# Two, four and three more places between reading an inverse back and transposing it, in a hybrid decoder step

## The chip, the cores and the metric

The kernel runs on one core of a Trainium2 chip. The metric is the device time in microseconds of one execution; a median over a few runs is compared. The profile is of one further execution.

## The reference

One layer of a decoder for 256 prompt tokens and 8 single new tokens: half-step SwiGLU, then two head groups side by side (sliding-window attention with sinks, and RWKV-7 time mixing), an output projection, a second half-step SwiGLU and a norm. All in float32.

```python
x = x + 0.5 * swiglu(rmsnorm(x, n1), f1g, f1u, f1d)
proj = rmsnorm(x, nm) @ w_in
o_att = attend(q, k, v, sinks)                    # window 128, 16 heads, 4 kv heads
for t in range(T):                                # RWKV-7, 16 heads of 64
    sa = S @ (-kk[t])
    S = S * exp(logw[t]) + outer(sa, kk[t] * a[t]) + outer(v[t], k[t])
    y[t] = S @ r[t]
x = x + concat(o_att, groupnorm_gate(y)) @ w_out
x = x + 0.5 * swiglu(rmsnorm(x, n2), f2g, f2u, f2d)
```

The kernel doesn't run the recurrence token by token for the prompt. It cuts 256 tokens into four pieces of 64. In a piece, the effect of the tokens on each other is a lower triangular system, so each head and piece needs the inverse of a unit triangular 64 x 64 matrix; its two 32 x 32 diagonal blocks are inverted by elimination, the block off the diagonal by two products.

## The kernel before, in words

**The stream of weight chunks.** All big products (gu and dn of both SwiGLUs, win, wout) go through `gemm`: 1304 chunks of 128 x 512 weights (some narrower). For each, the queue of SyncE (SP) loads `raw` (six buffers), ScalarE (ACT) rounds it to `hi`, VectorE (DVE) subtracts to get `lo` (four buffers of each; from the query tiles on, and for wout, every second `lo` is GpSimd's, POOL), and TensorE (PE) does twelve products of 128 x 264, three for each of four 128-column slices, into a bank `acc`. Buffers of `raw` come free with `lo`, those of `hi` and `lo` with the chunk's products.

**The mixing stage** (768 to 1180 us of the span) does win (38 tiles of four chunks) and wout. Everything else of the stage is written as generators, `tick`ed once after every chunk; a `yield` is one place in the program, and `pause(n)` is n places. They are:

- `prep`, for each pair of heads: decays, keys and the Gram products (`gm` is their masked copy, TensorE's products are called `kr,bk`), which SP writes to DRAM (`sa`). After that come transposes of `kr` and `bk` (L515, L522) and a product `uv,gm`.
- `chain`, for each of four batches of two pairs. It waits for its `prep`s; it reads the matrices back from `sa` into `X` with one matrix row group to a partition, and POOL copies to `Xt`; it pauses DWAIT = 8 places; 30 steps of elimination follow, two a place, each a product `st` and an addition to `Xt` on VectorE. The inverse is written to DRAM (`sb`, four writes, L580), and after one place read back into `TT` in the layout for products (four reads, L585; the first and third hold what is transposed). After DWAIT - 2 = 6 places VectorE transposes the two halves, `TN` from `TT` (L591). Then TensorE multiplies `TN,gm`, and `TT,zs`, ScalarE copies the results, TensorE multiplies `kr,TT`, then with `W` (L639) come products `BT,W`, `gm,W`, `uv,BT` and `gm,uv`; VectorE scales `N`; three steps of state (`Z`, `S`) follow, and a group norm into `y`.
- attention, softmax and the decode tokens' part, in the last third of the stage.

`mp()` gives the small products one of five PSUM banks (NM = 5), `acc()` one of three.

**What sets the order.** Each engine and each queue works in order. The program order is not the final order: a scheduler puts each instruction on its engine's queue by its own estimates, and moves instructions at high priority (the chunk preparation) ahead. `tc.issue_after(cuts[0])` keeps a step of elimination and each transpose behind the newest `lo` of VectorE. So a place more in one generator moves other generators' instructions too.

Of the kernel before, what the change touches and what calls it, by code (L numbers as in the profile page):

```python
# [30 lines left out]
NWARM = 10  # L31
NGM, NKR, NUV, NTT, NBT = 10, 5, 3, 2, 5
NSTEP = 2
DWAIT = (8, 8, 8, 8)
PW = (2, 1, 3, 2, 2)
ALPHA = math.exp(-0.5)
LKV = 26
# [10 lines left out]
def body(tc, I, O):  # L48
# [42 lines left out]
    def pause(n):  # L91
        for _ in range(n):
            yield

    with ExitStack() as ctx:
# [264 lines left out]
        def mixing_body(mx, n2, n3, XD):  # L360
# [3 lines left out]
            def ring(shape, tag, bufs):  # L364
                return mx.tile(list(shape), F32, tag=tag, bufs=bufs, name=uid(tag))
# [172 lines left out]
            def newbatch(i):  # L538
                bt = Batch()
                n = BATCH[i]  # L540
                bt.i, bt.n, bt.left, bt.p0 = i, n, n, sum(BATCH[:i])
                bt.KR, bt.bv = [None] * n, [None] * n
                bt.Gm = [[None, None] for _ in range(n)]
                bt.BT = [None] * n
                bt.UV = ring((P, 4, n, P), "uv", NUV)
                return bt

            def chain(bt):
# [15 lines left out]
                for h in range(2):  # L564
                    G.memset(TT[h * 64 + 32:h * 64 + 64, :, 0:32], 0.0)
                yield from pause(DWAIT[bt.i])
                for s in range(1, 31):
# [14 lines left out]
                for h in range(2):  # L582
                    for blk in range(2):
                        x = h * 64 + blk * 32
                        SP.dma_start(TT[x:x + 32, :, blk * 32:blk * 32 + 32],  # L585
                                     scr2[bt.i].rearrange("(h b m) (s t) -> h b s m t", h=2, b=2, s=32)[h, blk])
                yield from pause(DWAIT[bt.i] - 2)
                TN = ring((P, n * 4, 32), "TN", 1)
                for h in range(2):
                    with tc.issue_after(cuts[0]):  # L590
# [286 lines left out]
            for kind, i in SEQ:  # L877
                if kind == "b":
                    bt = newbatch(i)
                    for k in range(BATCH[i]):  # L880
                        p = bt.p0 + k
                        x = [shifted(2 + 3 * p + j, tmp()) for j in range(3)]
                        spawn(prep(p, bt, k, *x))
                    bat.append(spawn(chain(bt)))
                    bts.append(bt)
                    if len(bat) == len(BATCH):
# [206 lines left out]
```

## Time and profile before

| what | value |
|---|---|
| median of 3 runs | 2002.0 us (2001.74 to 2003.65) |
| the profiled execution, whole | 1999.97 us |
| its span | 1997.9 us |
| TensorE busy | 1967.1 us, 98% |
| VectorE, ScalarE, GpSimd busy | 65%, 53%, 17% |
| DMA | 358.24 MB, mean 179 GB/s |

In the rows, `acc<-s,hi` names the result and the operands of an instruction, buffer numbers left out. The time in brackets is how long the engine stood idle before a row, and who ended it. SPq is SyncE's queue, whose rows are DMA issues and not transfers. PEclk is the granted TensorE clock, 1.00 for full.

### The profile page before, as it was taken

What the parts mean: (1) busy time and instruction counts of PE and PEld (TensorE: products, weight loads), DVE (VectorE), ACT (ScalarE), POOL (GpSimd) and SP (SyncE); (2) the same over time, 40 slices, a digit from 0 to 9 for tenths busy, and PEclk for the clock granted to TensorE, in tenths of its full rate; (3) what the DMA queues carried; (4) which work ended last, traced back from release to release, by engine and by line L of the source; (5) the groups of instructions that cost most, each with busy time, mean ns of one, the idle gap of its engine ahead of it and who ended that gap; (6) DMA issues with size and microseconds to landing.
All of it is one profiled execution on the core that took longest, in us unless ns stands there. A gap on an engine that the chain in (4) does not pass through costs nothing.

```text
span 1997.9 us, 45891 instructions
## 1 busy us (share of the span) xinstructions
PE 1967.1 (98%) x17212; PEld 1937.1 (97%) x17212; DVE 1305.4 (65%) x2542; ACT 1067.7 (53%) x2127; POOL 344.9 (17%) x453
## 2 busy tenths in 40 slices
PE   9999999999999999999899999999999999999997
PEld 9999999999999999999788899999999999999997
DVE  5865555655556567789677676766666666666655
ACT  5644444444444456776556765654444444444445
POOL 0401001010010122221134553220101001010012
PEclk9999999999999999999899999999999999999999
DMA  7666666655556567554455546565666666666654
GB/s 231 178 192 193 183 193 191 182 184 177 187 177 184 182 196 222 164 158 124 132 156 144 162 143 196 174 182 175 193 186 191 182 191 192 183 191 181 197 177 144
DMA packets 224880, 358.24 MB, mean 179 GB/s; under 512 B 38264, under 2 KB 79888, under 8 KB 224656
## 3 DMA queue, kind: packets, MB, share of 16 engines
q1 hardware_dynamic: 218768, 349.20, 58.4%
q10 hardware_dynamic: 5888, 6.11, 1.0%
q8 instruction: 135, 2.21, 0.5%
q14 instruction: 89, 0.73, 0.1%
HBM read 347.06 MB, written 10.22 MB: 179 GB/s over the span
## 4 chain that ended last, share of the span: by engine, by line
PE 94%; DVE 2%; DMA 2%; ACT 1%; SPq 1%; issue 0%; POOL 0%; DVEq 0%; ACTq 0%; POOLq 0%
PE acc L74 86%; PE m L74 7%; DMA TT<-sb 1%; DVE Xt L58 1%; DVE lo L58 0%; DMA raw<-in_gu 0%; DMA sb<-Xt 0%; DVE st L58 0%; DMA raw<-in_win 0%; ACT t L68 0%; DVE y L58 0%; DMA s<-xsp 0%; ACT hi L127 0%; DVE gm L58 0%; PE m L522 0%
## 5 line engine op out<-in xcount | busy, mean ns | idle before, releaser
L127 ACT CAST hi<-raw 128x512 fp32r<-128x512 f32 (+2 forms) x1304 | 779.0, 601 | 813.3 <-PE acc L74 721.4
L58 DVE TENSOR_TENSOR lo<-raw,hi 128x512 fp32r<-128x512 f32 (+1 forms) x1248 | 857.2, 691 | 540.6 <-ACT hi L127 511.7
L74 PE MATMUL acc<-s,hi 128*128 128x264 f32 x5940 | 1112.5, 287 | 3.0 <-ACT s L917 2.4
L74 PEld LDWEIGHTS acc<-s,hi 128*128 128x128 f32 x5940 | 926.5, 189 | 9.7 <-ACT s L917 2.6
L74 PE MATMUL acc<-s,lo 128*128 128x264 f32 x2970 | 849.4, 287 | 0.0
L74 PEld LDWEIGHTS acc<-s,lo 128*128 128x128 f32 x2970 | 560.6, 189 | 3.0 <-issue 0.7
L74 PE MATMUL acc<-t,hi 128*128 128x264 f32 x2752 | 502.8, 284 | 0.0
L74 PEld LDWEIGHTS acc<-t,hi 128*128 128x128 f32 x2752 | 425.9, 188 | 0.0
L74 PE MATMUL acc<-t,lo 128*128 128x264 f32 x1376 | 388.6, 284 | 0.0
L58 POOL TENSOR_TENSOR t<-t,t 128x264 f32<-128x264 f32 (+1 forms) x148 | 151.1, 1021 | 1149.6 <-ACT hi L127 817.6
L74 PEld LDWEIGHTS acc<-t,lo 128*128 128x128 f32 x1376 | 258.1, 188 | 0.1
L74 PE MATMUL acc<-y,hi 128*128 128x264 f32 x648 | 124.1, 285 | 0.0
L74 PEld LDWEIGHTS acc<-y,hi 128*128 128x128 f32 x648 | 101.0, 188 | 0.2
L74 PE MATMUL acc<-y,lo 128*128 128x264 f32 x324 | 92.0, 284 | 0.0
L58 DVE TENSOR_TENSOR t<-acc,t 128x264 f32<-128x264 f32 x156 | 67.4, 432 | 36.8 <-PE acc L74 36.6
L58 POOL TENSOR_TENSOR lo<-raw,hi 128x512 fp32r<-128x512 f32 x56 | 73.8, 1319 | 65.9 <-ACT hi L127 38.5
L58 POOL TENSOR_TENSOR o<-o,o 128x264 f32<-128x264 f32 x43 | 36.4, 847 | 186.2 <-ACT o L68 182.2
L74 PE MATMUL acc<-o,hi 128*128 128x264 f32 x324 | 63.2, 285 | 0.0
L74 PEld LDWEIGHTS acc<-y,lo 128*128 128x128 f32 x324 | 60.9, 188 | 0.0
L61 DVE SCALAR_TENSOR_TENSOR s<-acc,s 128x264 f32<-128x264 f32 x96 | 40.6, 427 | 16.0 <-PE acc L74 15.5
L74 PEld LDWEIGHTS acc<-o,hi 128*128 128x128 f32 x324 | 50.2, 188 | 0.0
L74 PE MATMUL m<-s,hi 128*128 128x264 f32 x260 | 48.3, 285 | 0.0
(251 smaller groups left out, 1337.8 us busy)
## 6 DMA issues: line engine op xcount, KB each, us to landing
raw<-in_gu SPq DMA_DIRECT2D x688, 256.0 KB, 3.4
raw<-in_dn SPq DMA_DIRECT2D x224, 256.0 KB, 2.9
raw<-in_win SPq DMA_DIRECT2D x152, 256.0 KB, 3.5
raw<-in_dn SPq DMA_DIRECT2D x160, 192.0 KB, 2.7
raw<-in_wout SPq DMA_DIRECT2D x48, 256.0 KB, 3.5
raw<-in_wout SPq DMA_DIRECT2D x32, 128.0 KB, 3.3
s<-xsp SPq DMA_DIRECT2D x16, 132.0 KB, 3.9
ld<-in_sT SPq DMA_DIRECT2D x16, 128.0 KB, 3.5
```

What stands on the lines that cost most here:

```text
L58: return e.tensor_tensor(out=out, in0=a, in1=b, op=op)
L61: return V.scalar_tensor_tensor(out=out, in0=a, scalar=s, in1=b, op0=op0, op1=op1)
L74: TE.matmul(out, lhsT, rhs, start=start, stop=stop, **k)
L127: A.copy(hi[:, :w], raw[:, :w])
```

## The change

The pause between the four reads and the transposes has a table of its own, RWAIT, with 8, 10, 9 and 6 places in place of 6 in each batch.

```diff
-DWAIT = (8, 8, 8, 8)
+DWAIT, RWAIT = (8, 8, 8, 8), (8, 10, 9, 6)
...
-                yield from pause(DWAIT[bt.i] - 2)
+                yield from pause(RWAIT[bt.i])
                 TN = ring((P, n * 4, 32), "TN", 1)
                 for h in range(2):
                     with tc.issue_after(cuts[0]):
                         V.transpose(TN[h * 64:h * 64 + 32], TT[h * 64:h * 64 + 32, :, 0:32])
```

The scheduler makes more of it than a shift. The first place is batch 1 on VectorE, from the last step of the elimination (`Xt_12573`) to the transposes. Before:

```order
L58 TENSOR_TENSOR Xt_12573<-Xt_12573,st_13573 128x8
L58 TENSOR_TENSOR pj_10572<-acc_13673,rs 128x264
L58 TENSOR_TENSOR lo_13893<-raw_13891,hi_13892 128x512
L58 TENSOR_TENSOR lo_13972<-raw_13970,hi_13971 128x512
L591 STREAM_TRANSPOSE TN_13848<-TT_12582 32x256 x2
L58 TENSOR_TENSOR lo_14048<-raw_14046,hi_14047 128x512
```

After, the rows from that step on, and those up to the transposes:

```order
L58 TENSOR_TENSOR Xt_12573<-Xt_12573,st_13573 128x8
L58 TENSOR_TENSOR pj_10570<-acc_13341,rs 128x264
L58 TENSOR_TENSOR lo_13634<-raw_13632,hi_13633 128x512
...
L58 TENSOR_TENSOR lo_13850<-raw_13848,hi_13849 128x512
...
L58 TENSOR_TENSOR lo_13868<-raw_13866,hi_13867 128x512
L58 TENSOR_TENSOR XD<-t_13329 128x8
L58 TENSOR_TENSOR gm_13576<-m_13539,C 128x512
L58 TENSOR_TENSOR lo_13926<-raw_13924,hi_13925 128x512
L58 TENSOR_TENSOR lo_13964<-raw_13962,hi_13963 128x512
L591 STREAM_TRANSPOSE TN_13980<-TT_12582 32x256 x2
```

Between the two stood three rows, two of them `lo`; now there stand 36, with eleven `lo` and two reciprocals. The elimination ends at an earlier chunk (eight chunks), the transposes come one chunk later.

The second place is the same batch on SP's queue, the writes `sb` and the reads `TT`. Before:

```order
L509 DMA sa_10583<-gm_13576 32x4x32 x2
L580 DMA sb_10586<-Xt_12573 256x1x32 x4
L126 DMA raw_14305<-in_win 128x512
L561 DMA X_13654<-sa_10583 32x1024
L585 DMA TT_12582<-sb_10586 32x8x32 x2
L126 DMA raw_14349<-in_win 128x512
L585 DMA TT_12582<-sb_10586 32x8x32 x2
```

After:

```order
L580 DMA sb_10586<-Xt_12573 256x1x32 x2
L126 DMA raw_13830<-in_win 128x512
L580 DMA sb_10586<-Xt_12573 256x1x32 x2
L126 DMA raw_13848<-in_win 128x512
L585 DMA TT_12582<-sb_10586 32x8x32 x4
```

The reads stood behind the fifth and the sixth raw after that of the `lo` ahead of the transposes (`raw_13970`); now they stand behind `raw_13848`, three raws ahead of it. In batch 2 the queue has four writes, the load of the cached keys (`uv<-in_kc`, L815), one raw and then the four reads, five raws earlier than before, and both transposes follow the same chunk's `lo` as the first did; from the elimination's end to them VectorE has 27 rows, five of them `lo`, one a reciprocal, twelve of `Z` and `S`.

The third place is TensorE in batch 1, where `N` is read, with the last of the products `gm,uv` ahead. Before:

```order
L74 MATMUL m_14095<-gm_12494,uv_11359 64x64
L74 MATMUL acc_14249<-s_10205,hi_14306 128x264
L74 MATMUL acc_14249<-s_10206,hi_14306 128x264
L74 MATMUL m_14157<-N_13992,PT_13991 64x64 x2
L74 MATMUL m_14095<-kr_12303,N_13992 64x64 x2
```

After:

```order
L74 MATMUL m_14244<-gm_12494,uv_11359 64x64
L74 MATMUL acc_14583<-s_10120,hi_14632 128x264
...
L74 MATMUL acc_14583<-s_10291,hi_14664 128x264
L74 MATMUL m_14302<-N_14139,PT_14138 64x64 x2
L74 MATMUL m_14244<-kr_12303,N_14139 64x64 x2
```

Two chunk products stood between, now twelve. The batch's `TN,gm` products stand in one group with the next pair's `XD,ld`, `kr,bk`, `C,kr` and `C,bk`; `TT,zs`, `kr,TT`, `BT,W` and `N` follow two, four, five and six chunks behind them. In batch 0 the `TN,gm` products likewise stand in the group of the next pair's `XD,ld` and `kr,bk`, four chunks later than before; in batch 2 they come three chunks later, five chunks behind the `lo` that the transposes follow; in batch 3 eleven behind it. Batch 3's elimination starts two chunks later, and its reads stand one to two raws later. The instructions are the same ones, but for two of ScalarE's table loads fewer (31 for 33).

## The prediction

> **What bounds the kernel now.** I read the page first, then busy time and granted clock by stretch, then TensorE's idle rows in order of time, and last VectorE's and the DMA queue's rows around the transposition.
>
> ```profile
> span 1997.9 us, 45891 instructions
> PE 1967.1 (98%) x17212; PEld 1937.1 (97%) x17212; DVE 1305.4 (65%) x2542; ACT 1067.7 (53%) x2127; POOL 344.9 (17%) x453
> PEclk9999999999999999999899999999999999999999
> ```
>
> TensorE bounds the kernel. It is idle for 30.8 us of the span, so a change of order can win only a part of that, and the time that matrix products lose when the granted clock drops. The clock row has its one dip in the slice from 949 us on, which is in the mixing stage. By stretch (TensorE busy is the first number after the length, PEclk the granted clock):
>
> ```profile
> core 0: us, PE busy (x) PEld busy (x) DVE busy (x) ACT busy (x) POOL busy (x), PEclk, DMA share, GB/s
> 895.00:920.00 25.00, 23.85 (x429) 21.25 (x427) 22.71 (x71) 15.25 (x44) 5.12 (x15) 0.93 0.50 139
> 920.00:945.00 25.00, 25.00 (x204) 24.25 (x204) 21.94 (x57) 19.92 (x45) 3.81 (x11) 1.00 0.42 119
> 945.00:965.00 20.00, 16.89 (x204) 15.68 (x203) 11.70 (x33) 13.66 (x34) 2.77 (x12) 1.00 0.67 169
> 965.00:990.00 25.00, 20.57 (x356) 18.61 (x356) 22.51 (x76) 12.36 (x34) 5.02 (x13) 0.85 0.44 126
> 990.00:1015.00 25.00, 25.00 (x212) 23.65 (x209) 18.95 (x49) 18.29 (x41) 1.84 (x10) 0.94 0.38 109
> 1015.00:1040.00 25.00, 21.34 (x232) 19.94 (x231) 12.74 (x24) 10.01 (x27) 8.57 (x13) 0.93 0.65 175
> 1040.00:1070.00 30.00, 27.00 (x387) 24.62 (x387) 27.08 (x98) 16.95 (x42) 13.27 (x19) 0.89 0.42 125
> ```
>
> Two losses are to be seen. TensorE is idle for 1.15, 3.11, 4.43, 3.66 and 3.00 us in five of these stretches, and every such stretch, or the one behind it, runs below the full clock: length times (1 - clock) is 1.75, 3.75, 1.5, 1.75 and 3.3 us. These are the idle rows (in brackets the idle time ahead, and who ended it):
>
> ```profile
> 904.75 0.71 PE L74 MATMUL m<-t,C 128*128 128x280 f32 x2 [0.47 <-POOL shc L407]
> 906.38 0.60 PE L74 MATMUL m<-kr,TT 64*64 64x64 f32 x4 [0.35 <-ACT TT L621]
> 907.21 1.48 PE L74 MATMUL m<-kr,TT 64*64 64x64 f32 x52 [0.23 <-ACT TT L621]
> 962.45 0.22 PE L74 MATMUL m<-TN,gm 32*32 32x32 f32 x2 [1.72 <-DVE TN L591]
> 964.06 0.45 PE L74 MATMUL m<-TN,gm 32*32 32x32 f32 x30 [1.39 <-DVE TN L591]
> 982.03 1.15 PE L74 MATMUL m<-gm,uv 128*64 128x64 f32 x32 [0.84 <-DVE gm L58]
> 987.21 0.37 PE L74 MATMUL m<-N,PT 64*64 64x64 f32 x2 [3.59 <-DVE N L58]
> 1027.26 1.11 PE L522 MATMUL m<-C,bk 128*128 128x128 f32 x4 [3.66 <-DVE t L58]
> 1055.66 1.62 PE L74 MATMUL m<-s,o 64*128 64x256 f32 x6 [3.00 <-DVE st L58]
> ```
>
> That a lower clock is lost time is shown by the chain of work: a run of chunk products takes 0.122 us each before the first batch's stall (7.68 / 63) and 0.187 right behind the second's (4.87 / 26):
>
> ```profile
> 801.51 7.68 PE acc L74 x63
> 964.50 4.87 PE acc L74 x26
> ```
>
> So a stall in this stage costs its length and some 1.7 us behind it (3.4 us at half clock; 1.75 in two of the stretches above), or twice that.
>
> **The wait that the change is about.** VectorE's and the queue's rows, batch 0 (895), batch 1 (953 to 964) and batch 2 (1014 to 1027):
>
> ```profile
> 895.39 0.43 DVE L591 STREAM_TRANSPOSE TN<-TT 32x256 f32<-32x256 f32 x1 [2.35 <-DMA TT<-sb]
> 953.10 0.17 DVE L58 TENSOR_TENSOR Xt<-Xt,st 128x8 f32<-128x8 f32 x1
> 954.03 2.53 SPq L580 DMA_DIRECT2D sb<-Xt  x4
> 957.97 0.80 SPq L585 DMA_DIRECT2D TT<-sb  x2
> 959.31 0.92 SPq L585 DMA_DIRECT2D TT<-sb  x2
> 961.87 0.43 DVE L591 STREAM_TRANSPOSE TN<-TT 32x256 f32<-32x256 f32 x1 [6.37 <-DMA TT<-sb]
> 963.57 0.44 DVE L591 STREAM_TRANSPOSE TN<-TT 32x256 f32<-32x256 f32 x1 [1.27 <-DMA TT<-sb]
> 1014.55 0.17 DVE L58 TENSOR_TENSOR Xt<-Xt,st 128x8 f32<-128x8 f32 x1
> 1026.71 0.43 DVE L591 STREAM_TRANSPOSE TN<-TT 32x256 f32<-32x256 f32 x1 [3.75 <-DMA TT<-sb]
> ```
>
> From the last step of the elimination to the transpose that waits, the way through DRAM takes 961.87 - 953.27 = 8.6 us for the first half and 10.3 for the second in batch 1, and 12.0 in batch 2, where weight loads stand between the writes. VectorE stands still for 7.6 and 3.75 us of it, in order, with everything behind the transpose held: the next lo, the t, gm and N that TensorE asks for.
>
> **The change part by part.** A pause issues nothing, and no DMA or product is added or taken away, so nearly all of it is order. ScalarE loads its tables 31 times for 33, 1.28 us each, of time in which it is idle nearly half (53% busy): 0 on the end.
>
> ```profile
> 888.21 1.28 ACT L68 ACT_TABLE_LOAD   x1
> ```
>
> Batch 1 (+4). The orders above show the elimination's last step eleven lo ahead of the transposes, two before, and the four reads on the queue behind the raw of the lo that is four ahead of the transpose, where two of them were behind a raw whose buffer (one of six) the lo right ahead of the transpose sets free. Between the last step and the transpose VectorE now has eleven lo, two reciprocals and 23 smaller steps. By these rows (a lo lasts 0.68 us, the next starts 0.60 after it):
>
> ```profile
> 965.46 1.79 DVE L441 RECIPROCAL t<-m 128x264 f32<-128x264 f32 x1
> 968.66 0.68 DVE L58 TENSOR_TENSOR lo<-raw,hi 128x512 fp32r<-128x512 f32 x1
> 969.26 0.42 DVE L58 TENSOR_TENSOR t<-t,t 128x264 f32<-128x264 f32 x1
> 987.95 0.47 DVE L61 SCALAR_TENSOR_TENSOR S<-m,wc,Z 128x64 f32<-128x64 f32 x2 [0.36 <-PE m L74]
> ```
>
> 11 x 0.60 + 2 x 1.75 + 23 x 0.35 = 18 us, more than the way's 10.3. The wait goes: TensorE's 1.72 + 1.39 and the 1.7 of clock behind it, **-4.8**.
>
> The backlog of batch 1. In 965 to 990 VectorE is busy for 22.51 of 25 us, and TensorE waits 0.84 for gm and 3.59 for N, with only two chunk products between the products that feed N and those that read it. In the new order twelve chunk products stand there (12 x 0.122 = 1.5 us), TN, TT, W and N are spread over chunks, and the held-up 7.6 us are gone. I take both waits and the clock lost around them (3.75 + 1.5 less the 1.7 just counted, 3.5) as won: **-7.9**. The ends are 0, if the elimination of batch 2 alone makes N late, and 7.9; I take the upper, since the missing 7.6 us of VectorE exceed the 4.4 of waiting.
>
> Batch 2 (+3). Both transposes stand together after the lo they had before; the four writes and then the reads go out five raws earlier. VectorE has five lo, a reciprocal, twelve steps of Z and S and nine others from the last step on: 3.0 + 1.75 + 12 x 0.24 + 9 x 0.4 = 11.2 us, against 8.6 and 10.3. This is close, and the load of cached keys (L815) now stands between writes and reads, so up to some 3 us of VectorE's wait may stay; TensorE's products of TN come five chunks later, 5 x 12 x 0.122 = 7.3 us, which hides that. What TensorE waited for was t behind the transpose: 3.66 + 1.7, **-5.4**.
>
> The 3.00 us at 1055.66 and 3.3 of clock: VectorE is full there (27.08 of 30) with batch 3's elimination, N of batch 2 and q. The new order starts that elimination later and spreads it over more lo. Ends 0 and -6.4; nothing in the trace says which, so half, **-3.2**.
>
> Batch 0 (+2): its first transpose goes one lo and some 3.6 us of work later. VectorE's 2.35 us go, but no TensorE row waits for it, so 0; the second transpose may wait up to 1.7 us for its read (issued at 895.20, 3.94 to landing in the chain), with the chunks that are prepared ahead (four hi and lo buffers) as cover. Batch 3 (+0): its reads go out one to two raws later with its transpose in place; bounded by 0 and batch 2's 3.75 of VectorE, hidden, since TensorE's TN products stand eleven chunks behind it.
>
> What comes back: wherever products of a batch stand close together, short waits remain, as in batch 0, which never waited for TN: 0.47 + 0.35 + 0.23 and 1.75 of clock, 2.8 us. Batch 1 and 2 will each have one such: **+5.5**; ends 0 and twice that.
>
> Sum: -4.8 - 7.9 - 5.4 - 3.2 + 5.5 = -15.8. The profiled execution took 1999.97 us round its span of 1997.9, so 1984.2 there; it lies 2.0 below the median of the runs, 2002.0, from which I take the same: **1986.2 us**.
>
> The Trainium skill, TensorE: Matmul & The Clock Gate, "Why this matters for your kernels", has the clock fall for idle gaps of more than about 3 us between bursts of products. The trace agrees for the gaps of 3.00, 3.59 and 3.66 us, and not for batch 0, where 1.05 us in three pieces stand beside a clock of 0.93. By that rule batch 1's TN waits (1.72 and 1.39) would be worth 3.1 and what comes back 2.1, and the sum would be -17.5, that is 1984.5.
>
> **The rivals.**
>
> A, only the direct waits go. The backlogs before N and q are VectorE's load, not its delay, and stay. For it: 22.51 of 25 and 27.08 of 30. Against: the standing still ahead of the first. -4.8 - 5.4 + 5.5 = -4.7: 1997.3.
>
> B, nothing: the reads are moved along by the queue and land as late against the transpose as before. For it: batch 2's 11.2 against 10.3. Against: batch 1's 18. The waits of 3.1 and 3.7 stay: 2002.
>
> C, all goes, with nothing back: -4.8 - 7.9 - 5.4 - 6.4 = -24.5: 1977.5. For it: the stretch 920 to 945 is full at a clock of 1.00 while batch 0's recurrence runs.
>
> D, slower: the five banks that the small products share. In the new order batch 0's and batch 1's TN products stand in the same group as the next pair's kr,bk, and each takes a bank that the transposes of bk wait for; that is the wait of 1027.26. At both places 5.4, and N late behind each as in batch 1 before, 7.9: +26.6 against gross gains of 21.3, 2007.3. It decides from 21.3 us of new waits. Against it: in the stretches up to 895 such groups ran without idle time.
>
> **How the numbers follow.** About 0.2% (4 us) is what a measurement of this kernel can tell from no change. Forecast 0.48, A 0.22, B 0.10, C 0.13, D 0.07. Faster: 0.48, 0.13, two thirds of A (its 4.7 is near the bound) and 0.02 of B, 0.78; slower 0.06 of D and 0.02 of B, 0.08; the rest, 0.14, the same. Range: down to C's 1977.5, up to 1999 between A and B; outside lie most of B, D and a little of C.
>
> **What would show it.** Right: no idle time before TN for a DMA in batch 1 on VectorE, under 3 us in batch 2; no TensorE wait for TN; none over 1 us for N and for bk's transposes; a granted clock of at least 0.95 in the stretch of batch 1. Wrong: TensorE waits of over 3 us at new places in the mixing stage, for gm, t or N, with the dips of the clock behind them, or a load queue that waits for TensorE at L815 while chunks run out.

## The result and the profile after

The changed kernel takes 1983.66 us (median of 5 runs, 1982.53 to 1985.16) against 2001.74 for the kernel before (5 runs in turn, 1997.97 to 2003.65): ratio 0.9911, 95% interval 0.9899 to 0.9922, 18.1 us less. The forecast was 1986.2. The profiled execution took 1982.98 us around a span of 1981.2.

The page's first lines and its clock row, after:

```profile
span 1981.2 us, 45886 instructions
PE 1960.8 (99%) x17212; PEld 1931.5 (97%) x17212; DVE 1302.9 (66%) x2542; ACT 1064.1 (54%) x2125; POOL 347.8 (18%) x453
PEclk9999999999999999999999999999999999999998
```

The dip of the slice from 949 us on is gone. The same stretches as before, after the change:

```profile
895.00:920.00 25.00, 24.95 (x427) 23.35 (x427) 22.32 (x71) 16.88 (x48) 8.90 (x17) 1.00 0.62 173
920.00:945.00 25.00, 23.97 (x225) 22.56 (x222) 22.43 (x63) 18.44 (x42) 3.70 (x13) 1.00 0.41 103
945.00:965.00 20.00, 20.00 (x189) 18.81 (x188) 14.29 (x34) 11.89 (x26) 4.79 (x11) 1.00 0.69 193
965.00:990.00 25.00, 25.00 (x404) 23.59 (x404) 23.24 (x78) 19.34 (x52) 4.48 (x10) 1.00 0.58 154
990.00:1015.00 25.00, 23.78 (x277) 22.15 (x272) 20.63 (x48) 16.36 (x39) 7.47 (x15) 1.00 0.51 144
1015.00:1040.00 25.00, 25.00 (x317) 23.32 (x316) 16.89 (x53) 17.57 (x48) 11.69 (x18) 1.00 0.59 161
1040.00:1070.00 30.00, 26.40 (x312) 23.37 (x311) 23.24 (x89) 14.51 (x42) 8.82 (x12) 0.94 0.54 146
```

The clock is full in six of the seven, and TensorE is busy throughout where batch 1 had cost most (945 to 990). TensorE's idle rows of over 0.3 us between 768 and 1180 are four, where there were ten:

```profile
922.89 0.27 PE L74 MATMUL m<-N,PT 64*64 64x64 f32 x2 [1.03 <-DVE Xt L58]
994.36 0.27 PE L74 MATMUL m<-N,PT 64*64 64x64 f32 x2 [1.22 <-DVE Xt L58]
1048.64 0.27 PE L74 MATMUL m<-N,PT 64*64 64x64 f32 x2 [3.60 <-DVE st L58]
1091.50 0.39 PE L74 MATMUL acc<-s,hi 128*128 128x264 f32 x1 [0.83 <-POOL s L58]
```

All that are over 1 us are now waits for `N`, in each of batches 0 to 2. VectorE's transposes, batch by batch:

```profile
897.39 0.42 DVE L591 STREAM_TRANSPOSE TN<-TT 32x256 f32<-32x256 f32 x1
899.86 0.43 DVE L591 STREAM_TRANSPOSE TN<-TT 32x256 f32<-32x256 f32 x1 [1.71 <-DMA TT<-sb]
957.84 0.89 DVE L591 STREAM_TRANSPOSE TN<-TT 32x256 f32<-32x256 f32 x2
1008.73 0.89 DVE L591 STREAM_TRANSPOSE TN<-TT 32x256 f32<-32x256 f32 x2
1065.61 0.95 DVE L591 STREAM_TRANSPOSE TN<-TT 32x256 f32<-32x256 f32 x2 [0.37 <-DMA TT<-sb]
```

VectorE stands still 2.1 us behind the reads in all, 13.7 before. Where the time came from: the first product of the second SwiGLU, just behind the mixing stage, before and then after:

```profile
1227.16 0.41 PE L74 MATMUL acc<-y,hi 128*128 128x264 f32 x2
```

```profile
1211.51 0.41 PE L74 MATMUL acc<-y,hi 128*128 128x264 f32 x2
```

The stage had started 0.55 us later than before (long run of chunk products from 68.49, before from 67.94), so it is 16.2 us shorter, nearly all of the span's 16.7. TensorE's busy time in 768 to 1180, before and then after, shows how much of that is idle time:

```profile
768.00:1180.00 412.00, 393.61 (x4322) 366.41 (x4321) 313.57 (x855) 280.34 (x698) 125.52 (x225) 0.97 0.53 151
```

```profile
768.00:1180.00 412.00, 405.08 (x4455) 378.59 (x4454) 323.31 (x871) 285.93 (x718) 140.49 (x238) 1.00 0.56 158
```

405.08 - 393.61 = 11.5 us of idle time, which leaves about 4.7 of the 16.2 for everything else, the clock among it, if idle time counts in full. Length times (1 - clock) over the seven stretches falls from 12.0 to 1.8, by 10.2. Both can't count in full, and the runs don't settle how the 16.2 us divide: a slow period can hold idle time too, which is then counted twice.

### The profile page after: what moved, and what is told of

It is laid out like the page before. It is cut to its first block, busy times and chain, and to the rows that moved or that the text cites. A ratio compares the mean times of both kernels' runs of the same rounds, so it can differ in the third digit from the quotient of the medians.

```text
span 1981.2 us, 45886 instructions
## 1 busy us (share of the span) xinstructions
PE 1960.8 (99%) x17212; PEld 1931.5 (97%) x17212; DVE 1302.9 (66%) x2542; ACT 1064.1 (54%) x2125; POOL 347.8 (18%) x453
## 4 chain that ended last, share of the span: by engine, by line
PE 96%; DVE 1%; DMA 1%; ACT 1%; issue 0%; SPq 0%; POOL 0%; DVEq 0%; ACTq 0%; POOLq 0%
PE acc L74 88%; PE m L74 7%; DMA raw<-in_gu 1%; DVE lo L58 0%; DVE Xt L58 0%; DVE st L58 0%; DMA TT<-sb 0%; DVE y L58 0%; DMA raw<-in_wout 0%; DMA raw<-in_win 0%; ACT t L68 0%; PE m L786 0%; PE m L522 0%; ACT L68 0%; ACT hi L127 0%
```

## The experiments

Each kernel was timed in turn with the kernel before (medians of 4 to 11 runs; ratios with 95% intervals). The theory of the prediction is called **own place**: a batch's wait goes with more places of its own behind its reads, and what TensorE lost behind it was VectorE's standing still. Against it stood **order**: places of one batch move the next batch's elimination, and what counts is where the reads go out. Chunks are counted below by the `raw` loads from the program's start, from 0.

**One batch at a time.** `RWAIT` alone is changed, in this order: (8, 6, 6, 6), (6, 10, 6, 6), (6, 6, 9, 6) and (6, 10, 9, 6).

```diff
-DWAIT, RWAIT = (8, 8, 8, 8), (8, 10, 9, 6)
+DWAIT, RWAIT = (8, 8, 8, 8), (8, 6, 6, 6)
```

> Places 8, 6, 6, 6: only batch 0's two more. Theory 'own place' (a batch's wait goes because its own transposes come later): batch 0 never held up TensorE, so nothing: -2 to +2 us against before, and VectorE still waits some 7.6 us before batch 1's transposes. Theory 'order' (what counts is how many lo stand between the elimination's last step and the transposes, and batch 0's places move batch 1's elimination ahead: here it ends seven lo ahead of batch 1's transposes, where it was two): batch 1's VectorE wait falls below 2 us, no TensorE wait for TN, -12 to -18 us.

> Places 6, 10, 6, 6: only batch 1's four more. Own place: batch 1's waits go, -4.8 directly and -7.9 with the backlog. Order: batch 1's elimination still ends at the same chunk as before, three lo ahead of the transposes, and its reads stand where they stood, so VectorE still waits 5 to 7 us there; but TensorE's TN products come six chunks behind the transposes, where they stood one ahead of them, so TensorE itself doesn't wait: -5 to -12 us, and a VectorE wait that costs nothing.

> Places 6, 6, 9, 6: only batch 2's three more. Own place: batch 2's 3.7 us wait and the clock behind it go, -5.4. Order: nothing of batch 1 changes, and batch 2's elimination, reads and transposes stand at the same chunks as before, so -2 to +2 us with VectorE's waits of 7.6 and 3.7 us as they were.

> Places 6, 10, 9, 6: the change without batch 0's two. Own place: as the change, -16 to -19. Order: batch 1's reads stand as before (VectorE still waits 5 to 7 us there), so as with batch 1's four alone, -5 to -12 us: what batch 0's two add to the whole is the rest, 6 to 13.

Measured: 0.9935 (0.9922 to 0.9947) for batch 0 alone, 0.9966 (0.9954 to 0.9978) for batch 1 alone, 1.0006 (0.9997 to 1.0015) for batch 2 alone, 0.9916 (0.9903 to 0.9930) without batch 0: 13 us and 7 us faster, nothing, 17 us faster.

Own place falls. The batch for which it expected nothing gives the most, and batch 2's places alone give nothing. With batch 0's two places alone, batch 1's transposes stand at 947.78 and don't wait, and with batch 1's four alone they still do. VectorE, in the first and then in the second kernel:

```profile
947.78 0.89 DVE L591 STREAM_TRANSPOSE TN<-TT 32x256 f32<-32x256 f32 x2
```

```profile
962.74 0.43 DVE L591 STREAM_TRANSPOSE TN<-TT 32x256 f32<-32x256 f32 x1 [3.35 <-DMA TT<-sb]
963.80 0.44 DVE L591 STREAM_TRANSPOSE TN<-TT 32x256 f32<-32x256 f32 x1 [0.63 <-DMA TT<-sb]
...
1066.95 0.43 DVE L591 STREAM_TRANSPOSE TN<-TT 32x256 f32<-32x256 f32 x1 [3.03 <-DMA TT<-sb]
1070.66 0.43 DVE L591 STREAM_TRANSPOSE TN<-TT 32x256 f32<-32x256 f32 x1 [2.42 <-DMA TT<-sb]
```

In the orders, two places more in batch 0 end batch 1's elimination at lo 626 for 634, and its reads go out behind raw 634 for 641. Four places more in batch 1 leave that as it was; they move TensorE's `TN` products from chunk 635 to 643, so that TensorE no longer waits for `TN` though VectorE does. So either edit alone takes TensorE's wait for `TN` away. They also put batch 3's reads behind raw 685 to 687 with its transposes at lo 681: the wait moves there. Batch 2's three places mend that (reads behind 685, 17 us instead of 7). So the places of one batch are worth what they do to the next, and they don't add up: 13 + 7 + 0 against 18 for all. Order was right on this, but too low for the fourth kernel. That one leaves VectorE standing for 3.7 us in batch 1 and is as fast as the whole change within the intervals. So standing still can't be all.

**Standing still, by itself.** Before's numbers, without the reads: the inverse is missing from this kernel's result, and all else runs.

```diff
-for h in range(2):
-    G.memset(TT[h * 64 + 32:h * 64 + 64, :, 0:32], 0.0)
+G.memset(TT, 0.0)
...
-SP.dma_start(TT[x:x + 32, :, blk * 32:blk * 32 + 32], scr2[bt.i]...)     # four in a batch
```

> Before's numbers; the four reads of the returned inverse per batch are left out (its tile is set to zero instead), so the transposition waits for no DMA; the inverse in the result is missing. Standing still (what TensorE lost for gm, N and t around batches 1 and 2 comes from VectorE standing in order behind the reads): all of those waits go, 14 to 22 us faster. Own load (N and t are late because the elimination and the prep fill VectorE there, reads or not): only the direct TN waits and their clock go, 3 to 6 us faster, with waits of 3 us for N and t still there.

Measured: 1991.47, ratio 0.9948 (0.9934 to 0.9961), 10 us faster, between the two. No transpose waits, and yet TensorE waits longer for `N` of batch 1 than before (3.59):

```profile
977.03 1.15 PE L74 MATMUL m<-gm,uv 128*64 128x64 f32 x32 [1.60 <-DVE gm L58]
983.88 0.37 PE L74 MATMUL m<-N,PT 64*64 64x64 f32 x2 [5.26 <-DVE N L58]
```

So the wait for `N` doesn't need VectorE's standing still. (Leaving out the reads moves the order a little too: the largest piece in the table below has 18 steps for 16.)

**The same places for batch 1, reached another way.** Batch 0's elimination starts two places later, all numbers behind the reads stay 6.

```diff
-DWAIT, RWAIT = (8, 8, 8, 8), (8, 10, 9, 6)
+DWAIT, RWAIT = (10, 8, 8, 8), (6, 6, 6, 6)
```

> All four numbers behind the reads are 6 as before; instead batch 0's elimination starts two places later (10 for 8 ahead of it). Batch 1's elimination then ends at lo 625 for 634 and its reads go out behind raw 633 with the transposition at lo 633 (before: raw 641 and 642, lo 635 and 636). Order (what counts is how many raw loads lie between the reads and the lo that the transposition stands behind; up to 3 ahead cost nothing, 5 or 6 cost 4 to 8 us of VectorE): no wait in any batch, 11 to 17 us faster. Own place (a batch's wait goes only with more places of its own behind the reads): no change, within 3 us of before.

Measured: 1996.71, ratio 0.9975 (0.9965 to 0.9984), 5 us faster, between the two ranges. Batches 1 to 3 have no wait behind the reads, as order said (batch 0's has, 3.73 us), but there is the other wait again:

```profile
991.25 0.37 PE L74 MATMUL m<-N,PT 64*64 64x64 f32 x2 [5.17 <-DVE N L58]
```

This kernel and the one with batch 0's places alone have the same order around batch 1 (elimination to lo 625 or 626, reads behind raw 633 or 634, transposes at lo 633, `N` at lo 646). They differ in batch 2's elimination: behind one `lo` stand up to 19 of its 30 steps here, up to 9 there, and TensorE waits 5.17 and 1.33 us for `N` of batch 1. That is the third theory, **burst**: `N` is late by the steps that stand in one piece ahead of it. (TensorE's rows differ too, which is taken up below the table.) In the kernel before, the largest piece is 16 steps; VectorE has no `lo` between these rows, and `N` stands at the end of the steps:

```profile
975.52 0.68 DVE L58 TENSOR_TENSOR lo<-raw,hi 128x512 fp32r<-128x512 f32 x1
...
976.87 0.20 DVE L58 TENSOR_TENSOR st<-X,Xt 128x52 f32<-128x52 f32 x1
...
985.72 0.21 DVE L58 TENSOR_TENSOR Xt<-Xt,st 128x55 f32<-128x55 f32 x1
985.86 0.61 DVE L58 TENSOR_TENSOR kr<-m,kr 128x192 f32<-128x192 f32 x2
986.39 0.68 DVE L58 TENSOR_TENSOR N<-m,wc 128x512 f32<-128x512 f32 x1
```

A step is two instructions and some 0.5 us. In the changed kernel at most eight stand behind one `lo`.

**The change without batch 1's places**: `RWAIT` (8, 6, 9, 6).

> The change without batch 1's four places (8, 6, 9, 6). Raw of the reads less lo of the transposition: 0 in batch 1, -1 in batch 2, 2 to 3 in batch 3. Order: no DMA wait of VectorE above 0.5 us in any batch, 13 to 18 us faster than before, as the whole change. Own place: batch 1's 12.7 us (direct waits and backlog) stay, 3 to 6 us faster.

Measured: 1986.04, ratio 0.9925 (0.9912 to 0.9937), 15 us faster, with no wait behind the reads in batches 1 to 3, and 1.33 us for `N` of batch 1. Most of what the prediction gave to batch 1's four places comes without them.

**Batch 2's elimination four places earlier**, most of it in one piece: before's numbers, `DWAIT` (8, 8, 4, 8).

> Before's numbers behind the reads (6, 6, 6, 6); batch 2's elimination starts four places earlier (4 for 8). Batch 1 stands as before (reads behind raw 641, transposition at lo 635 and 636); batch 2's reads go out behind raw 651, its transposition stands at lo 653, so it does not wait, but 24 of its 30 steps now stand on VectorE behind one lo (16 before, 8 in the change), ahead of N of batch 1. Burst (N of a batch is late by the steps of the next batch's elimination that stand in one piece ahead of it: 8 or 9 steps 0.9 to 1.3 us, 16 steps 3.6, 18 or 19 steps 5.2): TensorE waits 6 us or more for N of batch 1, which eats what batch 2's reads give: between 3 us faster and 5 us slower. Reads alone (only VectorE's standing behind the reads counts): batch 2's 3.66 us and their clock go, 4 to 7 us faster.

Measured: 1994.61, ratio 0.9967 (0.9954 to 0.9979), 6.6 us faster. The wait for `N` grew, to a little less than expected, but the time came out as reads alone had it:

```profile
990.21 0.37 PE L74 MATMUL m<-N,PT 64*64 64x64 f32 x2 [5.56 <-DVE Xt L58]
...
1050.32 0.37 PE L74 MATMUL m<-N,PT 64*64 64x64 f32 x2 [4.25 <-DVE st L58]
```

The 3.66 us at batch 2's `C,bk` are gone. TensorE's busy time in 768 to 1180 rises by only 1.3 us (394.91 for 393.61). The profiled span is 5.8 us shorter (1992.1 for 1997.9), but 2.2 of that lie behind the mixing stage: the first product of the second SwiGLU comes only 3.6 us earlier (1223.60 for 1227.16). From there to the end the traces of all these kernels take between 768.5 and 772.0 us. Where the other two in the stage come from isn't settled. So the wait for `N` and what the reads cost are two things.

**Ten places in all batches**: `RWAIT` (10, 10, 10, 10).

> Ten places in all four batches. Raw of the reads less lo of the transposition: 0 or 1, -2, 0 or 1 in batches 1 to 3; most steps of the next batch's elimination behind one lo: 8, 7, 13. Reads and burst: no DMA wait of VectorE in batches 1 to 3 and N of batch 1 within 1.3 us, so as the change or up to 4 us more for batch 3's 13 steps: 1982 to 1988. Set of numbers (the gain hangs on two, four and three just so): 1990 or more.

Measured: 1983.23, ratio 0.9911 (0.9897 to 0.9924): as the change. No transpose waits anywhere; `N` of batch 1 waits 1.41 us, a little over what was expected. The gain doesn't hang on two, four and three. Nor is it measured by idle time alone: in 768 to 1180 TensorE is busy for 400.40 us here and 405.08 in the changed kernel, so it idles 4.7 us more, at the same time for the whole.

All kernels, by the size of batch 2's largest piece (counted in the orders), the waits of VectorE behind the reads in batches 1, 2 and 3, and TensorE's waits in us:

| kernel | steps | reads, batch 1 / 2 / 3 | `N` of batch 1 | at 1044 to 1060 | ratio |
|---|---|---|---|---|---|
| all ten | 7 | 0 / 0 / 0 | 1.41 | 3.30 | 0.9911 |
| the change | 8 | 0 / 0 / 0.4 | 1.22 | 3.60 | 0.9911 |
| without batch 0 | 8 | 3.7 / 0 / 0.9 | 0.87 | 3.20 | 0.9916 |
| batch 1 alone | 8 | 4.0 / 0 / 5.5 | 0.87 | 2.65 | 0.9966 |
| without batch 1 | 9 | 0 / 0 / 0 | 1.33 | 3.29 | 0.9925 |
| batch 0 alone | 9 | 0 / 0 / 0 | 1.33 | 3.37 | 0.9935 |
| before | 16 | 7.6 / 3.8 / 0 | 3.59 | 3.00 | 1 |
| batch 2 alone | 16 | 7.7 / 3.1 / 0 | 3.60 | 5.12 | 1.0006 |
| no reads | 18 | none | 5.26 | 2.98 | 0.9948 |
| elimination 0 later | 19 | 0 / 0 / 0 | 5.17 | 3.66 | 0.9975 |
| elimination 2 early | 24 | 7.4 / 0 / 0 | 5.56 | 4.25 | 0.9967 |

The wait for `N` of batch 1 goes with the piece and not with the reads: 0.9 to 1.4 us for 7 to 9 steps, 3.6 for 16, 5.2 to 5.6 for 18 and more. But the piece isn't all that differs between the two groups. Between the last `gm,uv` and `N` the traces of the first six kernels show eleven or twelve chunk products on TensorE, those of the last five two or three. And of the steps only those count that VectorE does behind this `gm,uv`, whose result `N` scales: three or four in the first six, five and a half in before and batch 2 alone, nine in no reads and elimination 0 later, ten of the 24 in elimination 2 early. The rows in the changed kernel, TensorE's and then VectorE's:

```profile
990.38 1.10 PE L74 MATMUL m<-gm,uv 128*64 128x64 f32 x32
```

```profile
991.51 0.20 DVE L58 TENSOR_TENSOR Xt<-Xt,st 128x35 f32<-128x35 f32 x1
...
993.53 0.68 DVE L58 TENSOR_TENSOR N<-m,wc 128x512 f32<-128x512 f32 x1
```

From the end of `gm,uv` to the first product of `N` the kernel before takes 4.03 us (983.18 to 987.21), of which chunk products fill 0.44; the changed one takes 2.88 (991.48 to 994.36), of which they fill 1.66. So of the 2.37 us by which this wait shrank, 1.15 come from the shorter way, with eight instructions of the elimination in it (1.45 us) for eleven (2.45), and 1.22 from the ten chunk products more. The wait for `gm` goes with neither: it is 0.8 to 1.6 us in every kernel without batch 1's own places, 0.99 in the two with short pieces, and gone in every kernel that has them.

At nine steps or fewer, all but one kernel gain 13 us or more; that one stands still in batch 3.

**Towards a faster version.** What is left is the wait of 3.60 us in batch 2, behind batch 3's elimination. Two edits were aimed at it: that elimination four places later, and the `lo` of the first four query tiles on VectorE.

```diff
-DWAIT, RWAIT = (8, 8, 8, 8), (8, 10, 9, 6)
+DWAIT, RWAIT = (8, 8, 8, 12), (8, 10, 9, 6)
```

> The change, and batch 3's elimination started four places later (12 for 8 ahead of it): it is spread over lo 667 to 677 with 4 steps for one lo at most (8 before). In the changed kernel TensorE still waits 3.60 us for N of batch 2 at 1048.64 behind steps of batch 3's elimination. Order: that wait shrinks by half or more, batch 3's reads stay 0 to 2 raws ahead of its transposition: 1979 to 1983 us, 1 to 5 us faster than the change. Rival: the steps only move against batch 3's own transposition, gm and N, and the same 3 us are lost there: 1983 to 1987.

```diff
-gemm(ps, I["win"][t], n2.xs, tick, share=t >= LKV + 4)
+gemm(ps, I["win"][t], n2.xs, tick, share=t >= LKV + 8)
```

> The change, with eight lo of the first four query tiles moved from GpSimd to VectorE. In the changed kernel four steps of batch 3's elimination, at 1030 to 1041, last 1.17 to 1.31 us for 0.2, and each ends with a lo of GpSimd that had started just before it; TensorE then waits 3.60 us for N of batch 2. The order around N of batch 2 stays (elimination at lo 668 to 677 for 667 to 675). Held up by GpSimd: the long steps go (one or none left before N), the N wait falls to under 2.5 us, 1 to 4 us faster than the change, 1979.5 to 1982.5. Load (VectorE is full there, and eight lo of 0.6 us are no less than four steps held for 1.0): the wait stays at 3 us or more, 1982.5 to 1987.

The later elimination: 1987.84, ratio 0.9935 (0.9923 to 0.9948), the wait still 3.45: the rival, and a little over its range. The edit didn't spread the elimination as the expectation says; in the order up to eight steps still stand behind one `lo`, as in the change. The second: 1983.79, ratio 0.9912 (0.9899 to 0.9926), no gain either (the time lies in the range of load), but the cause that it tests is shown. In the changed kernel, GpSimd's `lo` and then VectorE's steps:

```profile
1036.36 1.27 POOL L58 TENSOR_TENSOR lo<-raw,hi 128x512 fp32r<-128x512 f32 x1
...
1038.18 1.53 POOL L58 TENSOR_TENSOR lo<-raw,hi 128x512 fp32r<-128x512 f32 x1
...
1041.00 1.27 POOL L58 TENSOR_TENSOR lo<-raw,hi 128x512 fp32r<-128x512 f32 x1 [1.29 <-ACT hi L127]
```

```profile
1036.41 1.29 DVE L58 TENSOR_TENSOR Xt<-Xt,st 128x46 f32<-128x46 f32 x1
...
1038.49 1.31 DVE L58 TENSOR_TENSOR Xt<-Xt,st 128x66 f32<-128x66 f32 x1
1039.83 0.23 DVE L58 TENSOR_TENSOR st<-X,Xt 128x63 f32<-128x63 f32 x1
...
1041.12 1.23 DVE L58 TENSOR_TENSOR Xt<-Xt,st 128x57 f32<-128x57 f32 x1
```

Each long step starts within 0.4 us of a `lo` of GpSimd and ends with it. With the `lo` moved, two long steps are left for four before `N`, at the two `lo` that GpSimd still does, and the wait shrinks to 2.24 us:

```profile
1048.91 0.37 PE L74 MATMUL m<-N,PT 64*64 64x64 f32 x2 [2.24 <-DVE st L58]
1074.98 0.33 PE L786 MATMUL m<-C,t 128*128 128x128 f32 x1 [1.35 <-ACT t L68]
```

The 1.36 us won come back as a wait for `t` in the attention, while VectorE stands still behind batch 3's reads (2.27 and 1.69 us, so 4.0 and not the 5.9 of the next expectation). The last run gives batch 3 four places more for that: `RWAIT` (8, 10, 9, 10).

> As e10, with four more places in batch 3 too (8, 10, 9, 10): its transposition stands at lo 685 for 681, with the reads behind raw 685 to 687. In e10 VectorE stood still for 5.9 us behind those reads (2.27, 1.69 and a shorter one) and TensorE waited 1.35 us for ScalarE's t right behind. Theory (what e10 won at N of batch 2 it lost to this standing still): VectorE's wait for the reads falls under 2 us, TensorE's 1.35 goes, N of batch 2 stays near 2.2, 1979 to 1982.5. Rival: the time goes to another short wait of 1 to 2 us between the attention's parts, 1982.5 to 1986.

Measured: 1986.73, ratio 0.9920 (0.9907 to 0.9934). VectorE's wait behind the reads (1.1 us in all) and the 1.35 went, as expected, `N` stays at 2.20, and yet the time is a little over the rival's range. The rival's new waits are there, on TensorE:

```profile
1091.91 0.39 PE L74 MATMUL acc<-s,hi 128*128 128x264 f32 x1 [1.43 <-POOL s L58]
...
1162.25 0.39 PE L74 MATMUL acc<-s,lo 128*128 128x264 f32 x1 [0.79 <-POOL lo L58]
```

The first is 0.83 in the change, and the second isn't there. (The kernel with batch 3's elimination later has both too, 1.42 and 0.80.) With them TensorE's busy time in 768 to 1180 is that of the change (405.30 and 405.08). Of the 3.7 us between the two profiled spans, 2.2 have come about by the first product of the second SwiGLU (1213.67 for 1211.51) and the rest behind it; why isn't settled. No version beats the change.

## Why the prediction was right in sum, and wrong in its reasons

The forecast of 15.8 us less came to 18.1. By the prediction's own signs: no DMA wait ahead of `TN` in batches 1 and 2, no TensorE wait for `TN`, none for the transposes of `bk`, a clock of 1.00 in batch 1's stretch, all as said; no wait over 1 us for `N` was wrong, 1.22 and 3.60.

- Batch 1's direct waits (-4.8): gone, 3.1 us of them idle. The mechanism was partly wrong. The prediction read the earlier end of batch 1's elimination as the work of batch 1's places; it is that of batch 0's. Batch 1's own take TensorE's wait away by moving its `TN` products.
- The backlog of batch 1 (-7.9): 4.43 us of idle became 1.22. The step that failed is "the held-up 7.6 us are gone" as the cause. Without any standing still the wait for `N` was 5.26. About half of what went is the twelve chunk products that the prediction named (1.22 us more than before); the other half (1.15) is that batch 2's elimination is spread, 8 steps behind one `lo` for 16, so that fewer of them stand ahead of `N`. The prediction had named the end that came out of this ("if the elimination of batch 2 alone makes N late") and ruled against it by comparing sums, 7.6 of VectorE against 4.4 of waiting, where the order of the rows decides. The 0.84 for `gm` went with batch 1's own places.
- Batch 2 (-5.4): the 3.66 us are gone, but not by its own three places, which alone leave 2.78 there and bring 5.12 for `N`.
- The 3.00 us at 1055.66 (half, -3.2): taken for half won, and not won. It became 3.60 us for `N` of batch 2; only the clock there rose, 0.89 to 0.94.
- Batch 0 (0): by itself worth 13 us, beside the others 1 (0.9911 against 0.9916, inside the intervals). "No TensorE row waits for it" was true of batch 0 and said nothing of what its places move.
- What comes back (+5.5): short waits did (1.03 in batch 0 in place of its 1.05, 0.83 and 0.20 in the attention; the 1.22 is counted with the backlog), but none of the clock that was put to them: the stretches around 922 and 994 are at 1.00.
- Not foreseen: 2.39 us for ScalarE's `s` at 1106.48 and 0.63 at 1084.35 are gone.

```profile
1084.35 0.87 PE L74 MATMUL m<-t,s 128*64 128x256 f32 x8 [0.63 <-ACT t L68]
1106.48 0.63 PE L74 MATMUL acc<-s,hi 128*128 128x264 f32 x3 [2.39 <-ACT s L917]
```

By kind, the prediction's terms were 10.6 us of idle time and 5.1 of clock (8.6 gross, less 3.5 that was to come back); the stage lost 11.5, and 4.7 of everything else. Idle, term by term: 3.1 for 3.1, 3.2 for 4.4, 3.7 for 3.7, -0.6 for 1.5, -1.0 for -2.1, and 3.0 not foreseen. So it is partly luck that the sum came out: the 3.00 us stall that wasn't won was made up by two waits not foreseen. For the clock nothing so firm can be said. The 4.7 speaks for a gross term that was too large, made up by a return that didn't come; the 10.2 by granted clock speaks against it; and the kernel with ten places everywhere shows that idle time isn't lost time one for one. Of the rivals, A and B are out by their times, C expected 1977.5, and of D's new waits for banks there is no row among TensorE's idle ones.

## What to carry to other kernels

When a scheduler turns places into an order, compare the orders engine by engine before pricing an edit by the batch that it names: what a batch's places are worth may lie in the next batch, and edits that remove the same wait don't add up. A late operand has two possible causes on its in-order engine, standing still and a piece of lower-value work placed ahead, and how long it is waited for hangs as much on the work that the reader has in between. Listing the rows of both engines, from what the late instruction needs to what waits for it, tells these apart; a sum of busy time doesn't. A wait on an engine that isn't the bound is worth removing only if the bound's next request falls behind it: 3.7 us of VectorE's standing still cost nothing that could be measured (0.9916 against 0.9911, with intervals of some 0.0013 either way).

## What the runs showed of the hardware

In the changed kernel, an instruction of the elimination that VectorE starts while GpSimd does a `lo` (1.27 to 1.53 us) lasts 1.2 to 1.3 us for 0.2, until GpSimd's instruction ends. The Trainium skill, SBUF — State Buffer, "SBUF: two separate sides", describes an exclusive lock on a port pair that the two engines share, held for the whole instruction, which a VectorE operation with two operands in SBUF takes against a GpSimd operation that reads SBUF. The trace agrees, with these numbers, and so do the two long steps that were left with two `lo`.

The clock doesn't follow the length of the idle gap alone. In the traced run of the kernel without batch 0's places TensorE idles 3.20 us for `N`, at full clock; in that of the one with `lo` moved, 2.24 us (row above) stand in a stretch at 0.89. The row and its stretch in the first, and the stretch in the second:

```profile
1048.02 0.27 PE L74 MATMUL m<-N,PT 64*64 64x64 f32 x2 [3.20 <-DVE Xt L58]
```

```profile
1040.00:1070.00 30.00, 26.80 (x327) 24.01 (x326) 23.66 (x87) 17.25 (x47) 11.78 (x14) 1.00 0.49 142
```

```profile
1040.00:1070.00 30.00, 27.76 (x315) 24.56 (x314) 21.08 (x89) 14.06 (x37) 8.60 (x12) 0.89 0.46 129
```

The rule that the prediction weighed, of the Trainium skill's page TensorE: Matmul & The Clock Gate, "Why this matters for your kernels" (a fall for gaps of more than about 3 us), fits the changed kernel's own gaps: 1.03 and 1.22 at 1.00, 3.60 at 0.94. It doesn't fit these two. They are one execution each, and executions of one kernel differ: the four of the kernel without batch 0's places had a clock of 0.998, 0.996, 0.995 and 0.994 over the whole program, at 1981.38, 1986.17, 1983.53 and 1987.04 us, and the traced one is the first. What decides beside the gap isn't settled.

The loss comes in pieces of about 1.7 us. Length times (1 - clock), added up over windows of 5 us from 768 to 1180, gives 0 without batch 0's places, 1.7 in the change, 3.4 with batch 0's places alone, 5.1 with batch 1's alone, 6.8 with elimination 0 later and 12.0 before. So the prediction's unit for the clock behind a stall holds; which stalls bring one it couldn't tell.
